# An encoder layer with product-key experts: both segments through one input stage, gathers behind it, half of the one-hot factors on ScalarE, a batched end

## The chip, the core and the metric

The kernel runs on one core of a Trainium2 chip. A core has five engines: PE (TensorE: matmuls; its weight loads are counted apart as PEld), DVE (VectorE), ACT (ScalarE), POOL (GpSimd) and SP (SyncE, which only issues DMAs here). Each engine takes its own instructions in order and waits for the others at semaphores; DMA engines move data beside them. The metric is device time of one execution in microseconds (us), as the median over runs.

## What is computed

One layer of an encoder over two groups of tokens with shared weights: a prompt of 512 tokens (four tiles of 128) and a sample of 256 (two tiles), D = 1024, all in float32.

```python
h = rmsnorm(x, norm1_g)
qa, ka, va, qg, kg, vg, rg, lr, gl = split_in_proj(einsum('bsd,de->bse', h, w_in))
ya = rmsnorm(diff_attention(qa, ka, va, lam, rel_bias)) @ w_up_a        # 4 heads
yb = (rmsnorm(gla forward + gla backward) * silu(rg)) @ w_up_b          # 4 heads, chunks of 64
gates = sigmoid(gl)                                                     # 2 branches
x = x + (gates[0] * ya + gates[1] * yb) @ w_out
x = x + peer_ffn(rmsnorm(x, norm2_g))
x = x + (p_i @ ple_w) * sigmoid(rmsnorm(x, norm3_g) @ ple_gate_w)
y = rmsnorm(x, final_norm_g)

def peer_ffn(h):                    # 8 heads; 128 x 128 = 16384 experts u, v of 1024
    s = (h @ w_q) . sub_keys        # 8 heads x 2 halves x 128 keys
    idx, top = the 16 best sums of the two halves, for each token and head
    act = gelu(u[idx] . h)
    return sum over the 8 x 16 choices of softmax(top) * act * v[idx]
```

## The kernel before

Float32 operands of the large products are split into a high and a low part (`split`: the high part is a copy on ACT, the low part a subtraction on DVE or POOL), and `mm3` (lines 176 to 178) makes each product of three matmuls: high by high, low by high, high by low. `wchunk` loads a weight chunk of 512 KB on SP's queue and splits it.

**Input stage, 0 to 944 us.** The sample goes first, alone: attention (`attention`, one head after the other), gated linear attention (`linear_attention`), `merge` (branch gates times the two branches), `out_proj`, `norm2`, `queries`. Then `choose` picks 128 experts for each of the sample's tokens (`select`, DVE almost alone), 352 to 398 us. Meanwhile PE makes 11 of the prompt's 16 branch gates (`branch_gate`, into tiles named fill), which go to DRAM and come back in `merge`. The prompt then takes the same way from 398 to 944: attention, linear attention, merge, out_proj, norm2 with the products of the per-layer inputs (`ple_products`), queries. So w_in (40 chunks) and w_up (8) are loaded and split twice. Splits of weights are shared between DVE and POOL.

**Sample experts: gathers.** For the sample's two tiles the chosen rows of u and v are fetched: 512 indirect DMAs of 128 rows each (`fetch`, line 703, issued by POOL, tile name row); DVE takes a dot product with each u row tile (line 725) and adds each v row tile (line 734). The generator `gg` yields after each fetch, and `pace(n)` takes it n steps on: calls of `pace` in other code set where the gathers stand. They begin under the prompt's attention.

**Prompt experts: two loops over all 16384 experts, dense.** First loop (64 chunks of 128 experts, 944 to 1480 us): `up` multiplies a chunk of u with the 512 tokens (24 matmuls into tile pa), `gelu` (line 996, ACT) makes act, which goes to DRAM (line 1010). Beside it `outer_products` builds a table of gates: for each token, L is the one-hot row of its 128 first indices and R the one-hot row of its second indices times the gate, both by comparison with iota on DVE (lines 949 and 954); L by R (line 957, tile po) gives 128 x 128 gates of one token, which ACT copies out (line 958). A step handles four tokens; an iteration takes two or three steps. Second loop (32 blocks of four chunks, 1480 to 2577 us): the other 64 chunks of u, and in eight groups a block the product of act times gates with v; each block's groups pace 11 gathers. Inside both loops the order on PE, DVE, ACT and POOL is the order in which the code is written (`manual_schedule`).

**End, 2577 to 2673 us.** `finish_all` multiplies by ple_gate_w, adds, normalizes (`rsqrt_mean`, a chain of small DVE instructions, once for each tile), scales (line 1102) and stores.

Of the kernel before, what the change touches and what calls it, by code (L numbers as in the profile page):

```python
# [16 lines left out]
P = 128  # L17
# [92 lines left out]
def build(tc, A, O):  # L110
# [8 lines left out]
    pss = tc.alloc_tile_pool(name="pss", bufs=2, space=PSUM, side="right")  # L119
# [4 lines left out]

    def side_tile():
        return ps2.tile([P, 2, 512], F32, name="side", bufs=1)

    def fill_tile():
        return pss.tile([P, 512], F32, name="fill", bufs=2)

    def pair_tile():
        return psb.tile([P, 2, 512], F32, name="pair", bufs=1)
# [21 lines left out]
    nw = [0]  # L154
    wf = None
    wx = tc.alloc_tile_pool(name="wx", bufs=1, side="right")

    def wchunk(src, eng=None, base=False, own=None):
        raw = (own or wp).tile([P, 8, P], F32, name="raw", bufs=2 if own else 3)
        nc.sync.dma_start(raw, src)  # L160
        nw[0] += base
        pool = own or (wx if base and nw[0] % 3 == 2 else wp)
        hi = pool.tile([P, 8, P], F32R, name="whi")
        lo = pool.tile([P, 8, P], F32R, name="wlo")
        split(hi, lo, raw, eng or G)
        return hi, lo

    def half_unit(src, k, base=False, dve=False):
        wh, wl = wchunk(src[:, 4 * k:4 * k + 4].rearrange("p a b -> p (a b)").rearrange("p (a b) -> p a b", b=P),
                        V if k or dve else G, base)  # L170
        return [a.rearrange("p a b -> p (a b)").rearrange("p (a b) -> p a b", b=256) for a in (wh, wl)]
# [27 lines left out]
    class Seg:  # L199
        def __init__(self, t0, nt, xT):  # L200
            self.t0, self.nt, self.n, self.xT = t0, nt, nt * P, xT
            self.tiles = list(range(t0, t0 + nt))

# [7 lines left out]
    def norm1(sg, pool):  # L211
        n = sg.n
        acc = pool.tile([P, n], F32, name="sqa", bufs=1)
        xc = pool.tile([P, 8, n], F32, name="xc", bufs=1)
        for c in range(0, 8, 2):
            nc.sync.dma_start(xc[:, c:c + 2], A[sg.xT][:, c:c + 2])
        for c in range(8):
            if c == 0:
                S.activation(acc, xc[:, c], AF.Square)
            else:  # L220
                sq = pool.tile([P, n], F32, name="sq", bufs=2 if n < 512 else 1)
                S.activation(sq, xc[:, c], AF.Square)
                V.tensor_add(acc, acc, sq)

        def finish():
            ps = mm_tile()[:, :n]
            if last_pe[0] is None:
                T.matmul(ps, ones, acc, start=True, stop=True)
            else:
                with tc.issue_after(last_pe[0].ins):  # L230
                    T.matmul(ps, ones, acc, start=True, stop=True)
            rs = rsqrt_mean(pool, ps, D, n, "n1", acc)
            for c in range(8):
                V.scalar_tensor_tensor(xc[:, c], xc[:, c], g1[:, c:c + 1], rs, op0=OP.mult, op1=OP.mult)
                split(sg.hT[0][:, c], sg.hT[1][:, c], xc[:, c], G if c % 3 == 2 else V)

        return finish
# [5 lines left out]
    hps = tc.alloc_tile_pool(name="hps", bufs=1)  # L243
    SS.hT = [hps.tile([P, 8, SS.n], F32R, name=n) for n in ("hsh", "hsl")]
    SP.hT = HP
    g1 = load("g1", [P, 8], A["g1"])
    lp = tc.alloc_tile_pool(name="ln", bufs=1)
    norm1(SS, lp)()
# [28 lines left out]
    wf = tc.alloc_tile_pool(name="wf", bufs=2, side="right")  # L277
    outer = tc.alloc_tile_pool(name="outer", bufs=1, side="right")
    SS.oa = [outer.tile([P, 4, SS.n], F32R, name="oa" + x) for x in "hl"]
    SS.ogl = outer.tile([P, 4, SS.n], F32R, name="ogl")  # L280
# [6 lines left out]
    nproj = [0]  # L287
# [15 lines left out]
    def attention(sg, mid=None):  # L303
        nt, n = sg.nt, sg.n
        op = tc.alloc_tile_pool(name="oat", bufs=1, reuse_waits="tile", side="right")
        onat = [op.tile([P, 4, P], F32, name=f"on{t}") for t in range(nt)]
        ssq = op.tile([P, nt, 4], F32, name="ssqa")
        with tc.tile_pool(name="at", bufs=2, reuse_waits="tile") as ap:
            for h in range(H):
                if h == MID and mid is not None:  # L310
                    mid()
                tb = ap.tile([P, W_TB], F32, name="tb")
                src = tbd[:, h]
                nc.sync.dma_start(tb, bass.AP(tensor=src.tensor, offset=src.offset + 127,
                                              ap=[[4 * 1024 - 1, P], [1, W_TB]]))

                o = proj(sg, 3 * h)
                qs = [ap.tile([P, n], F32R, name=f"qs{c}") for c in range(2)]
                for c in range(2):
                    hi, lo = HALF[c], HALF[1 - c]  # L320
                    S.activation(qs[c][hi], o[hi], AF.Copy, scale=0.125)
                    V.scalar_tensor_tensor(qs[c][lo], o[hi], 0.125, qs[c][hi].bitcast(F32),
                                           op0=OP.mult, op1=OP.subtract)
                o = proj(sg, 3 * h + 1)
# [59 lines left out]
    def linear_attention(sg, early, late):  # L384
        nt, n = sg.nt, sg.n
        nck = n // 64
        with tc.tile_pool(name="gl", bufs=2, reuse_waits="tile") as gp:
# [123 lines left out]
            for h in range(H):  # L511
                split(sg.og[0][:, h], sg.og[1][:, h], ogs[h])
# [690 lines left out]
```

## Time and profile before

| | |
|---|---|
| runs | 2674.69, 2660.84, 2669.11 us; median 2669.11 |
| profiled execution | 2674.42 us; its span 2672.7 us, mean granted clock 0.961 |
| PE busy | 2498.7 us (93%), 12640 records |
| DVE busy | 2106.7 us (79%) |
| ACT busy | 976.2 us (37%) |
| POOL busy | 832.0 us (31%) |
| moved by DMA | 622.57 MB, mean 233 GB/s |

The span is the time between the first and the last instruction of the profiled execution; about 2 us lie around it. Busy shares are means over stages that differ: what a stage is worth is read from that stage. The granted clock (PEclk) is the share of TensorE's full speed that the chip gave; 1.00 is 2.4 GHz, 0.50 is 1.2 GHz.

### The profile page before, as it was taken

The page shows a single profiled execution, that of the slowest core. Times are in us where ns is not written, and L with a number is a line of the kernel's source. Part 1 is how long each engine was busy: PE and PEld are TensorE (multiplying, and loading weights), DVE is VectorE, ACT ScalarE, POOL GpSimd, SP SyncE. Part 2 cuts the span into 40 slices and gives each one's busy share as a digit, 9 for nine tenths or more (in the row PEclk, how much of TensorE's full clock was granted, in tenths as well). Part 3 has the DMA queues.
Part 4 walks back from the last instruction along what each step waited for, and adds up shares of the span by engine and source line. Part 5 has one row for each costly group of instructions (what it writes and reads, how often), then busy time and mean ns, then how long its engine had stood idle before and what let it go on. Part 6 is the DMA issues. An engine that isn't in the chain of part 4 may idle for free.

```text
span 2672.7 us, 35759 instructions
## 1 busy us (share of the span) xinstructions
PE 2498.7 (93%) x12640; PEld 2064.1 (77%) x12640; DVE 2106.7 (79%) x4419; ACT 976.2 (37%) x1649; POOL 832.0 (31%) x682
## 2 busy tenths in 40 slices
PE   7899999999978969999999899999999999999995
PEld 5779987667775858778788688888888888887785
DVE  4755698896876799999877688888888888887365
ACT  6754425654233223333333322322222322223133
POOL 2224332341244301111111244444443544442100
PEclk9989999999987989999999899999999999999998
DMA  7325556673877237667677899999999999996231
GB/s 245 110 92 181 162 166 206 223 253 101 297 282 246 80 103 240 220 204 238 221 251 261 301 330 321 314 318 320 319 319 318 309 333 315 322 317 237 80 107 59
DMA packets 238340, 622.57 MB, mean 233 GB/s; under 512 B 20193, under 2 KB 90977, under 8 KB 235857
## 3 DMA queue, kind: packets, MB, share of 16 engines
q1 hardware_dynamic: 148304, 292.05, 34.4%
q0 software_dynamic: 73728, 268.47, 28.2%
q10 hardware_dynamic: 16128, 59.78, 5.8%
q8 instruction: 99, 1.62, 0.3%
q14 instruction: 81, 0.66, 0.1%
HBM read 557.30 MB, written 62.91 MB: 232 GB/s over the span
## 4 chain that ended last, share of the span: by engine, by line
PE 76%; DVE 16%; DMA 3%; issue 3%; ACT 2%; SPq 0%; POOL 0%; ACTq 0%; DVEq 0%; POOLq 0%
PE po L176 10%; PE po L178 10%; PE po L177 10%; PE pa L178 7%; PE pa L176 7%; PE pa L177 7%; PE mm L176 4%; PE mm L177 4%; PE mm L178 4%; PE po L957 3%; DVE R L954 1%; DVE side L734 1%; DVE wlo L985 1%; DVE eq L669 1%; DMA pr<-in_pT 1%
## 5 line engine op out<-in xcount | busy, mean ns | idle before, releaser
L703 POOL DMA_INDIRECT row<-in_v,idx x256 | 250.2, 977 | 744.6 <-DVE side L734 443.5
L178 PE MATMUL pa<-hh,wlo 128*128 128x512 f32 x1024 | 411.5, 402 | 18.2 <-DVE wlo L985 18.1
L176 PE MATMUL po<-vh,wth 128*128 128x512 f32 x1024 | 404.3, 395 | 13.5 <-ACT wth L150 12.8
L176 PE MATMUL pa<-hh,whi 128*128 128x512 f32 x1024 | 415.9, 406 | 0.0
L151 POOL TENSOR_TENSOR wlo<-raw,whi 128x1024 fp32r<-128x1024 f32 x125 | 303.1, 2427 | 348.5 <-ACT whi L150 264.3
L177 PE MATMUL pa<-hl,whi 128*128 128x512 f32 x1024 | 410.1, 401 | 0.0
L178 PE MATMUL po<-vh,wtl 128*128 128x512 f32 x1024 | 403.4, 394 | 0.0
L177 PE MATMUL po<-vl,wth 128*128 128x512 f32 x1024 | 402.8, 393 | 0.2 <-DVE vl L151 0.2
L703 POOL DMA_INDIRECT row<-in_u,idx x256 | 262.1, 1024 | 447.3 <-DVE gj L725 337.3
L734 DVE SCALAR_TENSOR_TENSOR side<-row,dots,side 128x1024 f32<-128x1024 f32 x256 | 328.5, 1283 | 11.9 <-DMA row<-in_v,idx 8.0
L150 ACT CAST whi<-raw 128x1024 fp32r<-128x1024 f32 x216 | 223.1, 1046 | 260.2 <-PE mm L177 99.7
L725 DVE SCALAR_TENSOR_TENSOR gj<-row,side 128x1024 bf16<-128x1024 f32 x256 | 310.9, 1214 | 3.5 <-DMA row<-in_u,idx 0.9
L150 ACT CAST vh<-raw 128x1024 fp32r<-128x1024 f32 x128 | 133.9, 1046 | 490.9 <-PE po L178 396.5
L178 PEld LDWEIGHTS pa<-hh,wlo 128*128 128x128 f32 x1024 | 195.7, 191 | 69.8 <-DVE wlo L985 22.4
L176 PEld LDWEIGHTS po<-vh,wth 128*128 128x128 f32 x1024 | 194.4, 190 | 57.8 <-ACT wth L150 16.7
L151 DVE TENSOR_TENSOR vl<-raw,vh 128x1024 fp32r<-128x1024 f32 x128 | 156.0, 1219 | 102.1 <-ACT vh L150 100.8
L177 PEld LDWEIGHTS pa<-hl,whi 128*128 128x128 f32 x1024 | 195.9, 191 | 44.9
L176 PEld LDWEIGHTS pa<-hh,whi 128*128 128x128 f32 x1024 | 196.3, 192 | 44.2
L178 PEld LDWEIGHTS po<-vh,wtl 128*128 128x128 f32 x1024 | 194.3, 190 | 42.9 <-DVE wtl L151 2.5
L177 PEld LDWEIGHTS po<-vl,wth 128*128 128x128 f32 x1024 | 194.5, 190 | 42.0 <-DVE vl L151 1.4
L1147 DVE TENSOR_TENSOR x<-x,po 128x512 f32<-128x512 f32 x256 | 173.7, 682 | 62.9 <-PE po L178 48.7
L996 ACT ACTIVATE act<-pa 128x512 f32<-128x512 f32 x128 | 76.0, 596 | 394.6 <-PE pa L178 394.6
(403 smaller groups left out, 4883.6 us busy)
## 6 DMA issues: line engine op xcount, KB each, us to landing
raw<-in_uT SPq DMA_DIRECT2D x128, 512.0 KB
raw<-in_v SPq DMA_DIRECT2D x128, 512.0 KB
raw<-in_w_in SPq DMA_DIRECT2D x80, 512.0 KB
gd<-blk ACTq DMA_DIRECT2D x16, 2048.0 KB
gr<-gd SPq DMA_DIRECT2D x32, 1024.0 KB
raw<-in_w_q SPq DMA_DIRECT2D x32, 512.0 KB
ad<-act ACTq DMA_DIRECT2D x64, 256.0 KB
ar<-ad SPq DMA_DIRECT2D x64, 256.0 KB
```

Of the source, the lines that this page charges most:

```text
L150: S.copy(hi, src)
L151: ins = (eng or V).tensor_sub(lo, src, hi.bitcast(F32))
L176: T.matmul(out, lh, rh, start=(i == 0), stop=False)
L177: T.matmul(out, lh, rl, start=False, stop=False)
L178: last_pe[0] = T.matmul(out, ll, rh, start=False, stop=(i == n - 1))
L669: V.tensor_tensor(eq, places[:, hf * Q:hf * Q + Q, None].to_broadcast([P, Q, 16]), marks[:, None, :].to_broadcast([P, Q, 16]), op=op)
L703: G.indirect_dma_start(out=r, out_offset=None, in_=A[table], in_offset=bass.IndirectOffsetOnAxis(ap=idx[:, k:k + 1], axis=0))
L725: V.scalar_tensor_tensor(jk, r, 1.0, hq, op0=OP.mult, op1=OP.mult, accum_out=dots[:, k:k + 1])
L734: V.scalar_tensor_tensor(acc, r, dots[:, k:k + 1], acc, op0=OP.mult, op1=OP.add)
L957: T.matmul(tp[:, k * P:(k + 1) * P], Rs[k], L[:, k], start=True, stop=True)
L996: S.activation(act, o, AF.Gelu_apprx_tanh)
L1147: V.tensor_add(x2[t][:, q], x2[t][:, q], o)
```

## The change

Sample and prompt share one input stage: `proj` takes the segments to which a chunk applies and yields one product for each, so each chunk of w_in and w_up is loaded and split once. Head 0 of attention runs for the sample alone while the prompt's first norm is made; heads 1 to 3, linear attention (two chains that alternate at `yield`) and merge take both. The branch gates are made inside `merge`, and the way through DRAM is gone. All weight splits ahead of the second loop are on DVE. The gathers begin behind `choose`, which now stands behind the sample's queries and the prompt's norm2: one step at each `ple_products` step (6) and each of the prompt's query chunks (16), one or two for each iteration of the first loop (96), 12 or 13 for each block of the second. In the first loop the R factors of every second token come from ACT, as Abs and then Relu, and a step handles eight tokens. At the end the square is taken one tile later, and the first five tiles share one reciprocal root and one round of stores.

The core of the diff (the segments' loops around it, and the same instructions written for either segment, are left out):

```diff
-    def wchunk(src, eng=None, base=False, own=None):
...
+    def wchunk(src, eng=None):
+        raw = wp.tile([P, 8, P], F32, name="raw", bufs=3)
         nc.sync.dma_start(raw, src)
...
-        split(hi, lo, raw, eng or G)
+        split(hi, lo, raw, eng or V)
...
-    def proj(sg, i):
-        nproj[0] += 1
-        wh, wl = wchunk(A["w_in"][i], V if sg is SP or nproj[0] % 2 else G, True)
-        o = projT(sg, wh, wl)
-        if sg is SP:
-            pace(PB)
-        return o
+    def proj(segs, i):
+        wh, wl = wchunk(A["w_in"][i])
+        for sg in segs:
+            yield sg, projT(sg, wh, wl)
...
+    def merge():
...
+                for b in range(2):
+                    for sg, o in proj(SEGS, 24 + 2 * j + b):
+                        th[sg, b] = mp.tile([P, sg.n], F32, name="gt", tag="gt" + sg.x, bufs=3)
+                        S.activation(th[sg, b], o, AF.Tanh, scale=0.5)
+                wh, wl = wchunk(A["w_up"][j])
...
     def queries(sg, hT, keys, tv, ti, qp, o_ps, s_ps):
...
-            wh, wl = wchunk(A["w_q"][j], V if sg is SS and j % 2 else G, True)
+            wh, wl = wchunk(A["w_q"][j])
...
+            if sg is SP:
+                pace(PQ)
...
-    for i in range(NF):
-        branch_gate(i, wf, fill_tile(), G, wf)
...
+    with tc.tile_pool(name="at0", bufs=2, reuse_waits="tile") as ap:
+        attn_head(0, (SS,), ap, 1)
+        with tc.tile_pool(name="lnp", bufs=1, reuse_waits="tile") as lp:
+            norm1(SP, lp)
+    with tc.tile_pool(name="at", bufs=2, reuse_waits="tile") as ap:
+        attn_head(0, (SP,), ap, 1)
+        for h in range(1, H):
+            attn_head(h, SEGS, ap, 1)
...
+    out_proj(SS, sqs, np_)
...
+    norm2(SS, sqs, np_, hg, tp_tile)
+    out_proj(SP, sqp, np_)
...
+        queries(SS, hg, keys, tvs, tis, qp, mm_tile, tp_tile)
...
+        norm2(SP, sqp, np_, HP, tp_tile)
...
+        for k, t in enumerate(SS.tiles):
+            choose(t, tvs, tis, k, qp)
...
+        for _ in ple_products(pp):
+            pace(1)
...
         queries(SP, HP, keys, tv, ti, qp, o_tile, o_tile)
...
         def outer_products(t):
...
-                for q in range(TB // 4):
...
+                for q2 in range(TB // 8):
+                    sets = []
+                    for q in (2 * q2, 2 * q2 + 1):
...
+                        for k in (1, 3):
+                            n = n0 + k
+                            Rs[k] = gb.tile([P, P], F32, name="R", bufs=RB)
+                            S.activation(Rs[k], iota, AF.Abs, bias=sT[:, 1, n:n + 1], scale=-1.0)
+                            S.activation(Rs[k], Rs[k], AF.Relu, bias=sT[:, 2, n:n + 1], scale=sT[:, 3, n:n + 1])
...
+                        for k in (0, 2):
...
+                            V.tensor_scalar(Rs[k], iota, sT[:, 1, n:n + 1], sT[:, 2, n:n + 1],
+                                            op0=OP.is_equal, op1=OP.mult)
...
-                advance(ga, 128 * (i - A0 + 1) // n - 128 * (i - A0) // n)
+                advance(ga, 64 * (i - A0 + 1) // n - 64 * (i - A0) // n)
...
-            pace(1)
+            pace(1 + i % 2)
...
-                if not pace(2 if g in (1, 4, 6) else 1):
+                if not pace(2 if g % 2 == 0 or g == 5 and b % 2 else 1):
...
                     if h:
                         if u == 3:
+                            store(0, NT - 1)
+                        square(NT - 1, u, cs)
+            store(NT - 1, 1)
```

How it moves instructions, first on ACT in the middle of the first loop. whi is the high part of the next chunk, pa the chunk's product, act its gelu, ad its place in DRAM, po the outer products, blk the table's block. Before:

```order
L996 ACTIVATE act<-pa 128x512
L1010 DMA ad_9295<-act 128x512
L958 COPY blk<-po 128x128x4 x2
L980 CAST whi<-raw 128x1024
L996 ACTIVATE act<-pa 128x512
```

and with the change (R: the factor, sT: the index, the gate and the negated gate of each token):

```order
L955 ACTIVATE act<-pa 128x512
L969 DMA ad_8422<-act 128x512
L900 ACTIVATE R<-iota,sT 128x128
L901 ACTIVATE R<-R,sT 128x128
L900 ACTIVATE R<-iota,sT 128x128
L901 ACTIVATE R<-R,sT 128x128
L900 ACTIVATE R<-iota,sT 128x128
L901 ACTIVATE R<-R,sT 128x128
L900 ACTIVATE R<-iota,sT 128x128
L901 ACTIVATE R<-R,sT 128x128
L917 COPY blk<-po 128x128x4 x2
L939 CAST whi<-raw 128x1024
```

Between the store of act and the copies there are now four pairs, each with its second instruction reading what the first one wrote.

Second, PE around the choices of the sample's experts. Before, behind the sample's queries (tp<-keys,pq are their last scores; fill is a prompt's branch gate):

```order
L176 MATMUL fill<-hh,whi 128x512
L177 MATMUL fill<-hl,whi 128x512
L178 MATMUL fill<-hh,wlo 128x512
L580 MATMUL tp<-keys,pq 128x128 x2
L176 MATMUL fill<-hh,whi 128x512
```

and with the change (mm<-hgh is the sample's last query chunk, tp<-ident,ht the transposes of the prompt's norm2, pwh, pwl and prh the parts of the per-layer input's product):

```order
L173 MATMUL mm<-hgh,wlo 128x256
L579 MATMUL tp<-keys,pq 128x128 x4
L569 MATMUL tp<-ident,ht 128x128 x32
L171 MATMUL mm<-pwh,prh 128x512
L172 MATMUL mm<-pwl,prh 128x512
```

Where the matmuls of the branch gates stood, there are now the transposes of norm2 and then at once the products of the per-layer inputs.

## Rows read from the trace of the kernel before

**Rows 1.** The page, part 4: the chain that ended last, by engine.

```profile
PE 76%; DVE 16%; DMA 3%; issue 3%; ACT 2%; SPq 0%; POOL 0%; ACTq 0%; DVEq 0%; POOLq 0%
```

**Rows 2.** Busy times by stretch (us, PE, PEld, DVE, ACT, POOL, PEclk, DMA share, GB/s).

```profile
0.00:944.00 944.00, 854.73 (x4824) 702.15 (x4825) 701.65 (x1903) 442.65 (x878) 313.32 (x234) 0.94 0.56 188
352.00:398.00 46.00, 42.28 (x174) 34.10 (x173) 46.00 (x219) 10.37 (x15) 23.52 (x13) 0.93 0.45 149
840.00:944.00 104.00, 103.71 (x500) 86.38 (x501) 74.81 (x456) 32.04 (x48) 32.38 (x15) 0.98 0.30 96
944.00:1480.00 536.00, 500.45 (x2605) 418.48 (x2604) 475.42 (x1230) 189.79 (x277) 71.35 (x71) 0.96 0.66 220
1000.00:1300.00 300.00, 284.85 (x1480) 237.42 (x1479) 287.44 (x736) 109.28 (x159) 37.47 (x39) 0.97 0.67 222
1300.00:1450.00 150.00, 150.00 (x818) 127.97 (x817) 116.62 (x251) 55.18 (x82) 22.45 (x21) 1.00 0.73 246
1530.00:2430.00 900.00, 899.25 (x3924) 736.78 (x3923) 764.81 (x979) 257.09 (x333) 413.55 (x354) 1.00 0.92 319
1700.00:1750.00 50.00, 50.00 (x221) 41.08 (x220) 43.96 (x70) 11.75 (x15) 28.70 (x25) 1.00 0.97 343
```

**Rows 3.** Time line of ACT, one iteration of the first loop (start, us, instruction, [idle]).

```profile
1103.25 0.60 ACT L996 ACTIVATE act<-pa 128x512 f32<-128x512 f32 x1 [5.38 <-PE pa L178]
1103.87 0.33 ACTq L1010 DMA_DIRECT2D ad<-act  x1
...
1110.65 0.60 ACT L996 ACTIVATE act<-pa 128x512 f32<-128x512 f32 x1 [4.09 <-PE pa L178]
```

**Rows 4.** Time line of PE in the same iteration.

```profile
1103.05 1.95 PE L957 MATMUL po<-L,R 128*128 128x128 f32 x16
1104.75 0.48 PE L176 MATMUL pa<-hh,whi 128*128 128x512 f32 x1
```

**Rows 5.** Groups of DVE by line, 944 to 1480 (busy us, mean ns | idle before).

```profile
L954 DVE TENSOR_SCALAR R<-iota,sT 128x128 f32<-128x128 f32 x512 | 142.0, 344 | 2.5 <-PE po L957 2.5
...
L734 DVE SCALAR_TENSOR_TENSOR side<-row,dots,side 128x1024 f32<-128x1024 f32 x63 | 80.7, 1281 | 0.0
L985 DVE TENSOR_TENSOR wlo<-raw,whi 128x1024 fp32r<-128x1024 f32 x63 | 76.9, 1221 | 41.4 <-ACT whi L980 41.3
```

**Rows 6.** Groups of ACT by line and shape, 0 to 944.

```profile
L495 ACT ACTIVATE jk<-tp 128x128 f32<-128x128 f32 x24 | 6.8, 283 | 0.0
...
L432 ACT ACTIVATE t<-mm,ab 128x512 f32<-128x512 f32 x4 | 2.7, 683 | 0.7 <-PE mm L429 0.5 <-DVE qe L451 0.2
...
L432 ACT ACTIVATE t<-mm,ab 128x256 f32<-128x256 f32 x4 | 1.9, 470 | 1.4 <-DVE qe L451 1.1 <-PE mm L429 0.3
```

**Rows 7.** Time line of ACT, two neighbours that do not depend on each other.

```profile
182.43 0.27 ACT L493 COPY gn<-tp 128x128 f32<-128x128 f32 x1
182.59 0.28 ACT L495 ACTIVATE jk<-tp 128x128 f32<-128x128 f32 x1
```

**Rows 8.** Instructions on gathered rows alone (us, DVE, POOL, PEclk, DMA share, GB/s).

```profile
0.00:944.00 944.00, 158.41 (x264) 144.24 (x131) 0.94 0.56 188
944.00:1480.00 536.00, 84.23 (x79) 70.58 (x66) 0.96 0.66 220
1480.00:2440.00 960.00, 398.83 (x445) 297.46 (x315) 0.99 0.92 319
```

**Rows 9.** Time line of PE after two waits, 533 and 614 to 619 us.

```profile
533.25 0.50 PE L176 MATMUL mm<-hh,whi 128*128 128x512 f32 x1 [1.27 <-ACT lrT L401]
...
614.60 0.50 PE L176 MATMUL mm<-hh,whi 128*128 128x512 f32 x1 [1.70 <-DVE silu L426]
614.93 0.40 PE L177 MATMUL mm<-hl,whi 128*128 128x512 f32 x1
...
619.28 0.39 PE L177 MATMUL mm<-hl,whi 128*128 128x512 f32 x1
```

**Rows 10.** Time line of ACT: scaling of the last tile of six, 5.41 us apart.

```profile
2667.80 0.72 ACT L1102 ACTIVATE x<-x,rs 128x512 f32<-128x512 f32 x1 [2.87 <-DVE rs L196]
```

More of the change, by code (lines that the diff above doesn't have):

```diff
@@ L276, in build @@
     lp.release()
[L277 to L280, printed above, removed]
     def projT(sg, wh, wl):
@@ new lines, in linear_attention @@
+                    vn = {}
+                    for sg, o in proj(SEGS, 16 + 2 * h):
+                        vT = gp.tile([P, sg.n], F32, name="vgT", bufs=1)
+                        S.copy(vT, o)
+                        vn[sg] = tile_(sg, "vgn", [P, sg.nt, P])
+                        to_natural(vn[sg], vT, sg.nt)
+                    for sg, ps in proj(SEGS, 17 + 2 * h):
+                        og = sg.silu[:, h]
+                        S.activation(og, ps, AF.Tanh, scale=0.5)
+                        V.scalar_tensor_tensor(og, og, 1.0, ps, op0=OP.add, op1=OP.mult)
@@ new lines, in linear_attention @@
+                    chains = [gla_head(sg, h, gp, tile_, lrT[sg], qd[sg, h], kd[sg, h], vn[sg], scm, ssq)
+                              for sg in SEGS]
+                    while chains:
+                        chains = [c for c in chains if next(c, True) is None]
+            rs = rsqrt_mean(gp, ssq.rearrange("p a b -> p (a b)"), P, NT * 4, "gl")
+            rs3 = rs.rearrange("p (a b) -> p a b", b=4)
+            ogs = {}
+            for sg in SEGS:
+                for t in range(sg.nt):
+                    V.tensor_mul(sg.gn[t], sg.gn[t], rs3[:, sg.r0 + t, :, None].to_broadcast([P, 4, P]))
+                for h in range(H):
+                    tp = tp_tile()
+                    for t in range(sg.nt):
+                        T.transpose(tp[:, t * P:(t + 1) * P], sg.gn[t][:, h], ident)
+                    ogs[sg, h] = tile_(sg, ("t0", "t1", "qe", "ke")[h], [P, sg.n])
+                    V.scalar_tensor_tensor(ogs[sg, h], tp[:, :sg.n], ggla, sg.silu[:, h], op0=OP.mult, op1=OP.mult)
@@ L777, in build @@
     LB = 4
[L778 to L802 removed]
+    RB = 10
+    PO = 1
+    PQ = 1
+    SEGS = (SS, SP)
+    oat = tc.alloc_tile_pool(name="oat", bufs=1, reuse_waits="tile", side="right")
+    ssqa = oat.tile([P, NT, 4], F32, name="ssqa")
+    for sg in SEGS:
+        sg.on = [oat.tile([P, 4, P], F32, name=f"on{sg.x}{t}") for t in range(sg.nt)]
     ggla = load("ggla", [P, 1], A["ggla"])
@@ L1132, in prepare, with four_groups @@
             return ws
+        def four_groups(ws):
+            os_ = [o_tile() for _ in range(4)]
+            for k, (th, tl, vh, vl) in enumerate(ws):
+                for g in range(4):
+                    r, q = slice(DEN[g // 2] * P, DEN[g // 2] * P + P), slice(g % 2 * 512, g % 2 * 512 + 512)
+                    T.matmul(os_[g], th[:, r], vh[:, q], start=(k == 0), stop=False)
+                    T.matmul(os_[g], tl[:, r], vh[:, q], start=False, stop=False)
+                    T.matmul(os_[g], th[:, r], vl[:, q], start=False, stop=(k == VB - 1))
+            return os_
         fresh = {}
```

665 lines of the change are left out of this document (297 added, 368 removed).

## The prediction

> **What bounds the kernel now.** I read the chain of waits first, then the busy times by stage, then time lines of single iterations. The chain is TensorE's (PE) for three quarters, VectorE (DVE) takes 16%, ScalarE (ACT) 2% [rows 1]: the question is where PE waits, and ACT has room on average. By stage [rows 2], the input stage (0 to 944 us) is busy for 854.7 us at a granted clock of 0.94; the first loop (944 to 1480) is nearly full, with DVE at 287.4 of 300 us in its middle; in the second loop PE is busy in 899.3 of 900 us, DVE in 764.8, with the DMA engines at 0.92. So a gain is possible only ahead of 1480 and in the last 100 us, and the second loop can only lose.
>
> In one iteration of the first loop [rows 3], 7.40 us lie from one gelu to the next. ACT needs 0.60 for the gelu and 0.33 to issue the store, then nothing that PE needs at once. PE has eight outer products ready when the chunk's matmuls end: they start at 1103.05, and the next chunk starts at 1104.75, 1.50 us after the gelu started [rows 3, 4]. PE does not stand still here, because the factors were made ahead on DVE. That is the place that the change touches most.
>
> **First loop.** It removes from DVE 256 of the 512 R factors (half of 142.0 us, 71 us) and puts 512 activations on ACT [rows 5]. The order of ACT settles what they cost: each step's eight activations stand behind the gelu, the gelu waits for the end of the chunk, and PE's outer products wait for the activations before the next chunk may start. So ACT's work moves from beside PE to the path. Half of the factors come from an engine that is idle on average, at the one moment when PE needs it.
>
> The pair: Abs with one pointer operand takes 470 ns on 256 columns and 683 on 512, so 0.83 ns a column and 364 ns on 128 [rows 6]. Relu here has two pointers; a 128-column activation without one takes 283 ns [rows 6], so a pointer is about 81 ns and the Relu 445. The Relu reads what its Abs wrote, so I let these two not overlap; neighbours that don't depend on each other start 0.16 us apart at 0.27 long, an overlap of 0.11 [rows 7]. A pair is 0.364 + 0.445 - 0.11 = 0.70 us. ACT is free 0.95 us after the gelu starts (1104.20); four pairs bring the last factor at 0.95 + 4 x 0.70 + 0.11 = 3.86, and one matmul (1.70 / 8 = 0.21) ends the step at 4.07 in place of 1.50: 2.57 us more in each of 64 steps, +165. The Trainium skill (ScalarE: Activation LUTs, What ACT_TABLE_LOAD costs) prices an activation at 186 ns and 0.833 ns a column, 93 ns for each pointer, 93 ns of overlap; by it the pair is 0.77 us, and the sum would be 18 us more than by the rows. No table load is added: Abs and Relu follow a Tanh without one before, and both orders hold 30 loads.
>
> Given back is what DVE costs PE now: at the pace of 1300 to 1450 (818 matmuls in 150.0 us) the 1480 of 1000 to 1300 would take 271 us, so 29 go. DVE keeps 71 us less of factors and gets 30 more gathers (96 against 66) of some 1.28 us [rows 5, 8], 38 us, so it stays clear. Together +136. Bounds: if all eight activations stream 0.16 apart the last is there at 0.95 + 7 x 0.16 + 0.28 = 2.35, which makes +1.06 a step, +68 - 29 = +39; without overlap, and 0.1 us for each hand-over, the pair is 0.91 and the step +3.30, +211 with nothing given back. I take +136, since the first row of the pair is the same function with the same kind of operand.
>
> **Clock.** PE's first new wait in a step ends with the first pair, 0.95 + 0.81 = 1.76 us after the gelu starts, less one DVE-made product: about 1.6 us of idling in each iteration. A gap of 1.27 us was followed by matmuls at full clock, one of 1.70 by 12 steps in 4.35 us (614.93 to 619.28) [rows 9], where (7.40 - 1.70) / 24 = 0.237 us each gives 2.84: 1.5 us lost at the lower level of 1.2 GHz. 1.6 lies between the two gaps, so I charge half of the 61 iterations: +45, between 0 and +92.
>
> **Input stage.** Each w_in and w_up chunk is loaded and split once for both segments (48 loads of 512 KB fewer; also the 16 gates' way through DRAM and back), and 109 of 131 gathers leave 0 to 944 (131 there now [rows 8], 22 in the new order). They took 158.4 us of DVE and 144.2 of POOL; the splits that POOL did come to DVE, 1.22 us each [rows 5]. PE's own matmuls stay, so what can come back is its idle time, 944 - 855 = 89 us, and the clock's, 0.06 x 944 = 57 us, some 50 of it in matmuls: 140 at most. Most waits in the heads are chains through ACT and DVE that two interleaved segments cover only in part; I take half, -70. Against it stand three new waits. In 352 to 398 DVE works on the two choices for 46.00 us while PE fills 42.28 us of it with prompt gates [rows 2]; now nothing of PE's stands there but products that need a split queued behind the choices on DVE: +42, bare. In the prompt's queries DVE has 74.8 of 104 us; 16 splits (1.22) and 16 gathers (1.28) make it 115: +12. The sample's queries get 8 splits: +2. Sum -14, from -84 (all back) to +56 (nothing).
>
> **Second loop.** Gathers rise from 315 to 394, over 1097 us rather than 960: 9% more a microsecond. DMA share 0.92 becomes about 0.97, DVE's 0.85 about 0.89. At 0.97 (1700 to 1750) PE was busy in 50.00 of 50 us [rows 2], so this is nearly hidden: 0 at best; at worst one gather step of 1.28 us late in each of 32 blocks, +41, since the POOL split of the next chunk stands behind one gather more. I take +10, a quarter of that.
>
> **End.** The last tiles each wait 2.87 us for a reciprocal root [rows 10]; six become two: -12 (-8 to -15).
>
> **Sum:** 136 + 45 - 14 + 10 - 12 = +165 on the profiled 2674.4, so 2839. That execution lies 5 us above the median of 2669.1, so **2834 us** against the median, 6% slower.
>
> **Rivals.**
> *The input stage pays (faster).* PE becomes the bound from 0 to 944 and gives back all of it: -84. For: DVE loses 158 us of gathers there, PE's idle time is scattered through it, and the interleaving is aimed at the same waits. Against: the bare choices. It decides if the activations are cheap: 64 x (4 x pair - 0.23) - 29 - 84 - 2 is zero at a pair of 0.51 us, between my 0.70 and the 0.32 of neighbours. At 0.40 it is -27: 2642 us. Chance 0.12.
>
> *The clock falls in every iteration (slower still).* For: the gap of 1.70 that is followed by a fall. If the fall is as short as there, 61 x 1.5 = +92 in place of 45; if a whole chunk runs at the lower level, its 24 matmuls cost 5.7 us more, 61 x 5.7 = +348. Against: gaps up to 1.27 pass without one. Between these ends about 2950 us. Chance 0.16. The Trainium skill (TensorE: Matmul & The Clock Gate, A second HAM failure mode: psum-queue depth-cycling) describes a kernel whose short idling between groups of matmuls made the clock swing between its two levels; the trace shows falls behind single gaps, but no loop that repeats one, and by that page this rival would be the likelier one.
>
> *The second loop is bound by gathers.* DVE or DMA at their limit for part of the time: +41 in place of 10, with the rest as forecast: 2865. For: 0.92 is close. Against: 0.97 passed. Chance 0.06.
>
> *The factors' wait is hidden.* PE would need other work between a chunk and its products; the order shows none. With input as forecast the total would be -29 - 14 + 10 - 12, about 2624. Chance 0.01. Between the cases, an input gain that just pays for cheap activations, within 0.5% (some 13 us, about what this measurement can tell from no change): 0.05.
>
> **How the numbers follow.** The forecast keeps 0.60. Slower is forecast, clock and gathers, 0.82; same 0.05; faster 0.12 + 0.01. The forecast's own bounds: a cheap pair (-97) with half of the input's remaining gain (-35) is 132 below it, a dear pair (+75) with every clock fall (+47) 122 above, 2702 to 2956; the top goes on to where the second rival's middle lies. So the range is **2700 to 2980**, which leaves out most of the first rival and the upper end of the second.
>
> **What would show it.** Right: in the first loop a step of about 10 us from gelu to gelu, with PE waiting some 2 us for ACT's R in each; pairs of 0.7 us; PE nearly still for 40 us at the choices; the input stage ending close to 944; the second loop as long as before, at a DMA share near 0.97; two waits for a root at the end. Wrong: a first loop under 560 us (activations cheap or covered), an input stage under 880, PE gaps in the second loop, or a granted clock under 0.8 in the first loop, which would be the second rival.

## The result and the profile after

The changed kernel takes 2983.39 us (2982.25 to 2983.52, 4 runs) against 2666.16 of the kernel before (2660.84 to 2674.69): ratio 1.1186, 95% interval 1.1153 to 1.1218, 317 us slower. The direction was forecast; the size, 165 us, was half of it, and 2983 lies 3 us above the range. The profiled execution of the changed kernel has a span of 2980.5 us, 308 more than the 2672.7 of the kernel before; the profiles divide these 308 us.

The chain that ended last (page, part 4) now has 12% of "issue" and 8% of ACT; in [rows 1] these were 3% and 2%:

```profile
PE 61%; DVE 14%; issue 12%; ACT 8%; DMA 3%; POOL 2%; ACTq 1%; SPq 0%; POOLq 0%; DVEq 0%
```

Busy times by stretch of the changed kernel (us, PE, PEld, DVE, ACT, POOL, PEclk, DMA share, GB/s), which answer to [rows 2]: the input stage, in it linear attention, the choices, the products of the per-layer inputs and the prompt's queries, then the first and the second loop:

```profile
0.00:1000.00 1000.00, 864.62 (x4828) 708.66 (x4829) 556.88 (x1651) 395.88 (x829) 30.93 (x58) 0.91 0.27 86
233.20:469.80 236.60, 202.22 (x1084) 155.03 (x1082) 114.64 (x240) 111.16 (x246) 5.38 (x19) 0.84 0.10 30
802.00:850.00 48.00, 7.20 (x29) 5.05 (x28) 47.27 (x229) 6.57 (x12) 6.85 (x7) 0.55 0.24 80
850.00:895.00 45.00, 22.79 (x71) 14.95 (x71) 23.97 (x33) 10.36 (x18) 2.39 (x3) 0.76 0.40 133
895.00:1000.00 105.00, 104.11 (x504) 85.50 (x505) 94.75 (x461) 30.84 (x46) 14.34 (x18) 1.00 0.48 165
1000.00:1769.00 769.00, 600.13 (x2631) 475.58 (x2629) 471.23 (x1138) 390.74 (x789) 100.43 (x100) 0.91 0.53 176
1769.00:2892.00 1123.00, 1070.63 (x4596) 870.23 (x4596) 961.98 (x1195) 312.90 (x406) 528.96 (x454) 0.97 0.91 320
```

Here the first loop ends with its last chunk matmul and the second with its last product with v. By the same marks the loops of the kernel before end at 1487 and 2570 (not 1480 and 2577, as above):

```profile
944.00:1487.00 543.00, 507.45 (x2634) 424.13 (x2633) 475.42 (x1230) 189.79 (x277) 71.35 (x71) 0.96 0.66 220
1487.00:2570.00 1083.00, 1065.21 (x4598) 867.47 (x4597) 869.27 (x1103) 307.81 (x403) 447.29 (x377) 0.98 0.85 293
```

So the 308 us lie in four places. The input stage ends at 1000 instead of 944 (+56). The first loop takes 769 instead of 543 (+226). The second loop lasts 1123 where it was 1083 (+40). From there to the end it is 89 against 103 (-14). The number of PE's records is the same (12640 in both); its waits and its clock changed.

An iteration of the first loop, ACT's time line of the changed kernel (start, us, instruction, [idle before]), against [rows 3]:

```profile
1303.55 0.60 ACT L955 ACTIVATE act<-pa 128x512 f32<-128x512 f32 x1 [4.26 <-PE pa L173]
1304.18 0.33 ACTq L969 DMA_DIRECT2D ad<-act  x1
1304.55 0.40 ACT L900 ACTIVATE R<-iota,sT 128x128 f32<-128x128 f32 x1 [0.40 <-DVE wlo L944]
1304.99 0.49 ACT L901 ACTIVATE R<-R,sT 128x128 f32<-128x128 f32 x1
1305.39 0.39 ACT L900 ACTIVATE R<-iota,sT 128x128 f32<-128x128 f32 x1
...
1307.44 0.49 ACT L901 ACTIVATE R<-R,sT 128x128 f32<-128x128 f32 x1
1307.85 1.26 ACT L917 COPY blk<-po 128x512 f32<-128x512 f32 x2
...
1314.13 0.60 ACT L955 ACTIVATE act<-pa 128x512 f32<-128x512 f32 x1 [4.08 <-PE pa L173]
```

and PE in the same iteration, against [rows 4]:

```profile
1303.35 0.38 PE L914 MATMUL po<-L,R 128*128 128x128 f32 x2
1305.53 2.95 PE L914 MATMUL po<-L,R 128*128 128x128 f32 x14 [1.80 <-ACT R L901]
1308.23 0.48 PE L171 MATMUL pa<-hh,whi 128*128 128x512 f32 x1
```

From gelu to gelu it is 10.58 us, 7.40 before. ACT stands idle for 4.1 to 4.3 us while PE works on the chunk, then does 3.4 us of factors while PE waits: after one product PE idles 1.80 us for the first pair, and the next chunk starts 4.68 us after the gelu instead of 1.50. PE's waits by cause, 984 to 1782 us (total, times, longest), have one leader:

```profile
PE po L914 <- ACT R L901: 118.4, 62, 2.6
```

### The profile page after: what moved, and what is told of

It is laid out like the page before. It is cut to its first block, busy times and chain, and to the rows that moved or that the text cites. A ratio compares the mean times of both kernels' runs of the same rounds, so it can differ in the third digit from the quotient of the medians.

```text
span 2980.5 us, 35546 instructions
## 1 busy us (share of the span) xinstructions
PE 2606.8 (87%) x12640; PEld 2124.9 (71%) x12640; DVE 2041.7 (69%) x4112; ACT 1133.9 (38%) x2112; POOL 660.3 (22%) x611
## 4 chain that ended last, share of the span: by engine, by line
PE 61%; DVE 14%; issue 12%; ACT 8%; DMA 3%; POOL 2%; ACTq 1%; SPq 0%; POOLq 0%; DVEq 0%
PE po L171 7%; PE po L173 7%; PE po L172 7%; PE pa L171 6%; PE pa L172 6%; PE pa L173 6%; PE mm L171 3%; PE mm L172 3%; PE mm L173 3%; ACT R L901 2%; POOL row L704 2%; PE po L914 2%; DVE wlo L153 1%; ACT R L900 1%; DVE gj L726 1%
## 5 line engine op out<-in xcount | busy, mean ns | idle before, releaser
L704 POOL DMA_INDIRECT row<-in_u,idx x256 | 251.9, 984 | 1004.1 <-DVE gj L726 724.6
L171 PE MATMUL pa<-hh,whi 128*128 128x512 f32 x1024 | 428.4, 418 | 0.0
L171 PE MATMUL po<-vh,wth 128*128 128x512 f32 x1008 | 397.7, 395 | 24.5 <-ACT wth L152 18.0
L172 PE MATMUL pa<-hl,whi 128*128 128x512 f32 x1024 | 418.2, 408 | 0.0
L173 PE MATMUL po<-vh,wtl 128*128 128x512 f32 x1008 | 396.3, 393 | 0.1
L153 DVE TENSOR_TENSOR wlo<-raw,whi 128x1024 fp32r<-128x1024 f32 x109 | 132.8, 1220 | 279.4 <-ACT whi L152 276.0
L914 PE MATMUL po<-L,R 128*128 128x128 f32 x1024 | 205.2, 328 | 133.4 <-ACT R L901 118.4
L152 ACT CAST whi<-raw 128x1024 fp32r<-128x1024 f32 x171 | 176.5, 1047 | 304.5 <-PE mm L172 160.7
L914 PEld LDWEIGHTS po<-L,R 128*128 128x128 f32 x1024 | 160.3, 215 | 180.7 <-ACT R L901 174.1
L171 PEld LDWEIGHTS pa<-hh,whi 128*128 128x128 f32 x1024 | 203.7, 199 | 45.6
```

What stands on the lines that cost most here:

```text
L152: S.copy(hi, src)
L153: ins = (eng or V).tensor_sub(lo, src, hi.bitcast(F32))
L171: T.matmul(out, lh, rh, start=(i == 0), stop=False)
L172: T.matmul(out, lh, rl, start=False, stop=False)
L173: last_pe[0] = T.matmul(out, ll, rh, start=False, stop=(i == n - 1))
L704: G.indirect_dma_start(out=r, out_offset=None, in_=A[table], in_offset=bass.IndirectOffsetOnAxis(ap=idx[:, k:k + 1], axis=0))
```

## The experiments

**One: the factors back on DVE.** Nothing else is undone; steps of eight tokens and the ring of ten tiles stay.

```diff
-                        for k in (1, 3):
...
-                            S.activation(Rs[k], iota, AF.Abs, bias=sT[:, 1, n:n + 1], scale=-1.0)
-                            S.activation(Rs[k], Rs[k], AF.Relu, bias=sT[:, 2, n:n + 1], scale=sT[:, 3, n:n + 1])
...
-                        for k in (0, 2):
+                        for k in range(4):
```

> The changed kernel with all four R factors of a group made on VectorE again; the step of eight tokens, the ring of ten R tiles and everything else stay. Theory W (ScalarE's eight activations stand between the gelu and PE's products, so their 3.3 us are on the path in every step): an iteration goes from 10.58 back to some 7.4 us, the first loop from 768 to 545 to 580 us (VectorE then has about 542 us of work in it), total 2983 down to 2770 to 2810 us. Rival (the step of eight tokens and the smaller ring hold PE up, whoever makes the factors): iteration stays above 9.5 us, total above 2930 us.

Measured: 2776.35 us, 207 less than the changed kernel. The first loop is down to 568 us although DVE is busy in 518 of them (e1_dve by stretch):

```profile
999.00:1567.00 568.00, 513.96 (x2628) 427.52 (x2626) 517.90 (x1394) 189.49 (x277) 101.68 (x100) 0.95 0.70 240
```

So the step of eight, the ring and the 30 gathers more account for at most the 25 us that are left to the 543 before; no run separates them.

**Two: the same activations, ahead of the gelu.** The generator yields between factors and products, and the factors of a step are asked for before the gelu is written.

```diff
                         sets.append((q, L, Rs))
+                    yield
                     tps = []
...
+            if m:
+                advance(ga, 1)
             act = gelu(o)
             nc.scalar.dma_start(ad[i // VB][:, i % VB], act)
...
+                advance(ga, 2 * m - 1)
```

> The changed kernel with the same 512 activations, but each step's factors are written ahead of the gelu, into the 4 us in which ScalarE waits for the chunk; the products stay behind the gelu. Theory W (the place of the activations, not their number): iteration 7.4 to 7.6 us, no wait of PE for R, granted clock of the first loop back from 0.91 to 0.96 or more, total 2745 to 2790 us. Rival (ScalarE's throughput or VectorE's operand sharing: the activations are too much work wherever they stand): iteration above 9 us, total above 2880 us.

Measured: 2765.98 us, 217 less than the changed kernel with the same 512 activations. ACT's time line (e2_ahead) shows the first and the last of the eight in the hole that was idle, and the gelu 7.41 us after the one before:

```profile
1065.53 0.60 ACT L956 ACTIVATE act<-pa 128x512 f32<-128x512 f32 x1 [0.80 <-PE pa L173]
...
1068.75 0.40 ACT L900 ACTIVATE R<-iota,sT 128x128 f32<-128x128 f32 x1
...
1071.64 0.49 ACT L901 ACTIVATE R<-R,sT 128x128 f32<-128x128 f32 x1
1072.94 0.60 ACT L956 ACTIVATE act<-pa 128x512 f32<-128x512 f32 x1 [0.80 <-PE pa L173]
```

So it was where the work stood, not how much. The loop takes 557 us, though, not less than the 543 before. Against experiment one, which has the same steps and gathers, what DVE gave up bought 11 us.

**Three: half of ACT's work left out.** Without the Relu the factors are not the one-hot rows.

```diff
-                            S.activation(Rs[k], Rs[k], AF.Relu, bias=sT[:, 2, n:n + 1], scale=sT[:, 3, n:n + 1])
```

> The changed kernel without the second activation (the Relu that turns the distance into the gate) of each ScalarE factor: this part of the one-hot factors is left out. Theory W: 4 x 0.41 = 1.64 us less in each of 64 steps, -105 us, and up to 45 more where PE's first wait of 1.80 us falls to 1.39 and the granted clock no longer falls: 2830 to 2880 us. Rival (PE pays for the handovers from ScalarE, not for its work): less than 30 us, above 2950 us.

Measured: 2856.32 us, 127 less. The usual iteration falls from 10.58 to 8.94 us: 105 us in 64 steps. That this is the 4 x 0.41 of my expectation is luck: the four Abs alone take 1.28 us where the eight activations took 3.38, so ACT became 2.10 us shorter, and 1.64 of it reached PE (e3_norelu, ACT):

```profile
1105.48 1.28 ACT L900 ACTIVATE R<-iota,sT 128x128 f32<-128x128 f32 x4 [0.40 <-ACT act L954]
```

The other 22 are mostly clock. PE's waits in the two kinds of iteration (e3_norelu; in every fourth, ACT also issues a store of the table between gelu and factors):

```profile
1105.93 1.83 PE L913 MATMUL po<-L,R 128*128 128x128 f32 x14 [1.27 <-ACT R L900]
...
1133.22 1.83 PE L913 MATMUL po<-L,R 128*128 128x128 f32 x14 [1.76 <-ACT R L900]
```

In none of the 51 iterations that have one of these waits and no other does the clock fall. In the changed kernel the two waits are 1.80 and 2.28 us. Behind 1.80, in the iteration shown above, the chunk's matmuls start 0.23 to 0.24 us apart; behind this 2.28 they do not (PE, changed kernel):

```profile
1104.85 3.25 PE L914 MATMUL po<-L,R 128*128 128x128 f32 x14 [2.28 <-ACT R L901]
...
1108.33 0.63 PE L172 MATMUL pa<-hl,whi 128*128 128x512 f32 x1
1108.76 0.63 PE L173 MATMUL pa<-hh,wlo 128*128 128x512 f32 x1
...
1110.38 0.40 PE L171 MATMUL pa<-hh,whi 128*128 128x512 f32 x1
```

They stand 0.43 us apart, the level of 1.2 GHz, until 1110.38. The longer wait comes with the 0.46 us that ACT's queue needs for the store at 1103.37. But its length alone does not decide: elsewhere in the same loop the clock falls behind 1.80 (matmuls 0.43 us apart) and stays up behind 2.28 (0.23):

```profile
1388.18 3.25 PE L914 MATMUL po<-L,R 128*128 128x128 f32 x14 [1.80 <-ACT R L901]
...
1391.66 0.63 PE L172 MATMUL pa<-hl,whi 128*128 128x512 f32 x1
...
1554.92 2.95 PE L914 MATMUL po<-L,R 128*128 128x128 f32 x14 [2.28 <-ACT R L901]
...
1557.94 0.40 PE L172 MATMUL pa<-hl,whi 128*128 128x512 f32 x1
```

Of the changed kernel's 55 iterations with no other wait, 24 contain a stretch at the lower level: 10 of the 14 with the longer wait (2.28 to 2.57) and 14 of the 41 with 1.80. Such an iteration is 0.6 to 1.4 us longer than one with the same wait and no fall, some 26 us together.

**Four: 32 gathers more in the first loop.**

```diff
-            pace(1 + i % 2)
+            pace(2)
```

> The changed kernel with two gathers in every iteration of the first loop instead of one and two in turn: 32 gathers come out of the second loop. Theory D (the 15.4 and 3.1 us that PE waits at 2820 us for the last tile's transposes are gathers that were not done when the loop ended): these waits go, the second loop ends 15 to 20 us earlier, total 2963 to 2970 us. Rival (that wait is the normal finishing of the last tile, as the 4 us in the kernel before, or the gathers cost the first loop as much): total within 5 us of 2983.

Measured: 2958.69 us, 25 less, a little more than the 13 to 20 expected. In the changed kernel PE waited at the end of the second loop for the last gathered rows, twice, before it could turn the sample's tiles (PE):

```profile
2834.99 1.94 PE L569 MATMUL pt<-ident,h 128*128 128x128 f32 x8 [15.43 <-DVE h L996]
2840.01 1.94 PE L569 MATMUL pt<-ident,h 128*128 128x128 f32 x8 [3.07 <-DVE h L996]
```

With 32 fewer gathers in the second loop (e4_pace2) the first of these is 4.97 us and the second is gone, as in the kernel before, where PE waited 4.1 us there:

```profile
2764.11 1.94 PE L569 MATMUL pt<-ident,h 128*128 128x128 f32 x8 [4.97 <-DVE h L996]
```

and the first loop is about as long as it was, 772 us.

**Five: the kernel before without fill work.** One number: none of the prompt's gates is made early.

```diff
-    NF = 11
+    NF = 0
```

> The kernel before, with none of the prompt's 16 branch gates as fill work (11 of them were): all are made at the end of the prompt's linear attention. Theory C (the input stage of the change is slower because gates that filled PE's waits have gone, not because the segments are merged): the choices stand bare, 38 to 42 us, and the fills that lay in other waits come back on the path, together 40 to 65 us more before the first loop, total 2708 to 2735 us. Rival (the merging itself, or the splits that left POOL, makes the input stage slower): less than 15 us, total below 2685 us.

Measured: 2719.12 us, 52 more than the kernel before (ratio 1.0193, 1.0159 to 1.0228), without any merging. PE now waits through the choices as in the changed kernel (e5_nofill, PE):

```profile
402.10 0.77 PE L340 MATMUL pair<-kd,qs 128*128 128x512 f32 x1 [45.39 <-DVE qs L322]
```

The changed kernel has the same hole, in two pieces (PE):

```profile
849.03 0.79 PE L171 MATMUL mm<-pwh,prh 128*128 128x512 f32 x1 [33.22 <-ACT prh L152]
863.81 0.80 PE L172 MATMUL mm<-pwl,prh 128*128 128x512 f32 x1 [13.98 <-DVE pwl L153]
```

The first names ACT, whose casts (pwh, prh) are short; in its queue they stood behind the second choice's exponential, which had waited for DVE (ACT):

```profile
847.22 0.31 ACT L693 ACTIVATE g<-g 128x128 f32<-128x128 f32 x1 [22.10 <-DVE g L692]
...
848.37 0.61 ACT L152 CAST prh<-pr 128x512 fp32r<-128x512 f32 x1
```

**Six: the end alone,** `finish_all` of the changed kernel in the kernel before.

```diff
+                        if k:
+                            square(k - 1, u, cs)
...
+                            store(0, NT - 1)
+                        square(NT - 1, u, cs)
+            store(NT - 1, 1)
```

> The kernel before with the changed end alone (square one tile later, first five tiles share one root and one round of stores). Forecast of the sum: four waits of 2.87 us for a root go, -12 us (-8 to -15), total 2652 to 2660 us against some 2668. Rival (the stores at once cost as much as the roots did): within 3 us of the kernel before.

Measured: 2653.97 us, ratio 0.9953 (0.9931 to 0.9976), 13 us less. Six waits of 2.87 us for a root [rows 10] are two; ACT's time line of the changed kernel shows the same pair:

```profile
2969.43 2.19 ACT L1041 ACTIVATE x<-x,rs 128x1024 f32<-128x1024 f32 x2 [3.40 <-DVE rs L191]
2974.89 0.72 ACT L1038 ACTIVATE x<-x,rs 128x512 f32<-128x512 f32 x1 [2.87 <-DVE rs L191]
```

**Seven: gates inside linear attention.** Eight of the 16 gates of both segments are made between the steps of the chains and kept in DRAM until merge.

```diff
                     while chains:
                         chains = [c for c in chains if next(c, True) is None]
+                        step += 1
+                        if step in (2, 4):
+                            early_gate()
```

> The changed kernel with 8 of the 16 branch gates of both segments made between the steps of the linear attention's chains, and kept in DRAM until merge. Theory C (PE idles 31.6 us and runs at a granted clock of 0.85 in the 227 us of linear attention because nothing of its own fills the chains): that stretch grows by less than the gates' 8 x 24 x (0.236 + 0.125) = 69 us which leave merge, total 2983 down to 2938 to 2960 us. Rival (the chains are bound by VectorE and ScalarE, which the gates also need): less than 10 us.

Measured: 2952.68 us, 31 less (two runs, 12.6 us apart); in the trace the input stage ends at 970 instead of 1000. Linear attention (e7_gates) takes 268 us instead of 237. One gate of each segment already stood there in the changed kernel, so seven more, 7 x 24 x 0.361 = 61 us of matmuls, went in for 31, and the clock there is 0.94 instead of 0.84:

```profile
231.00:499.00 268.00, 243.45 (x1418) 193.48 (x1416) 124.26 (x247) 124.73 (x268) 5.26 (x19) 0.94 0.17 54
```

**Eight: the choices between the query chunks.**

```diff
             if sg is SP:
-                pace(PQ)
+                advance(picks, 2)
...
-            pace(1 + i % 2)
+            pace(2)
```

> The changed kernel with the choices of the sample's experts taken in steps between the prompt's query chunks, the products of the per-layer inputs ahead of them, no gather before the first loop and two in each of its iterations. To be held against e4_pace2 (2958.7 us), which also has two. Theory C (the 47 us in which PE waits behind the choices are a matter of order): PE's wait goes, VectorE in the prompt's queries gets 47 us of choices for 20 us of gathers and becomes the bound there by some 15 us, total 2915 to 2940 us. Rival (VectorE's work only moves the wait into the queries): total above 2950 us.

Measured: 2947.09 us, 12 less than e4_pace2, short of what I expected and between the two ranges. The hole of 47 us is gone, but the first loop starts at 996 us, 2 earlier than in e4_pace2. The rival was the right one for this stage: the queries take 145 us instead of 105, and PE waits in them for splits that queue behind choices (e8_cover, PE's waits from 800 to 1000, and the stretch):

```profile
PE po L173 <- DVE wlo L153: 31.6, 3, 17.2
```

```profile
851.00:996.00 145.00, 110.41 (x502) 89.06 (x503) 122.96 (x615) 31.38 (x47) 0.14 (x1) 0.89 0.18 58
```

The choices are DVE's work: beside queries whose splits are DVE's too they did not hide, beside gates with their splits on POOL, in the kernel before, they did. Of the 12 us some 5 lie in the first loop; the rest I did not follow up.

**Nine: the kernel before with the changed outer products alone** (the diff of `outer_products` and its calls, and RB).

> The kernel before with the changed outer products alone (half of the R factors on ScalarE behind the gelu, steps of eight tokens, ring of ten); input stage, gathers and end as before. Theory W: an iteration goes from 7.41 to 10.6 us, the first loop from 536 to 755 to 775 us, total 2880 to 2910 us: this part alone is some 230 of the change's 317 us. Rival (the first loop's loss needs the change's other parts, its two gathers an iteration or the splits on VectorE): total below 2840 us.

Measured: 2891.43 us, ratio 1.0843 (1.0807 to 1.0879), 224 more. The wait is the same without the rest of the change (e9_factors, PE, 944 to 1710):

```profile
PE po L968 <- ACT R L955: 118.0, 62, 2.5
```

**Ten: three edits together** in the changed kernel: two, four and seven.

> The changed kernel with three edits together: factors ahead of the gelu (e2_ahead, -217), two gathers in every iteration of the first loop (e4_pace2, -25), eight gates inside linear attention (e7_gates, -31). If these are separate places on the path they add: 2710 us (2700 to 2730), still above the kernel before, by the bare choices (47 us). Rival (they share a cause, so part is counted twice): above 2740 us. Other rival (one chunk load for both segments pays once the covers are back): below 2670 us.

Measured: 2716.78 us, ratio 1.0188 (1.0158 to 1.0218). The single edits add to 273 us, together they gave 267: three separate places on the path. What is left to the kernel before is not the bare choices alone, though the 49 us are near their 47: between the profiled executions, 43 us apart, the input stage is 26 us longer (it ends at 970), the first loop 20 (563 against 543), the second 11, and the end is 14 shorter.

**Eleven: gathers off one short stretch of the kernel before.** On top of six, the gathers between the prompt's norm2 and its queries go (27 by the calls of `pace`, not the 30 of my expectation), 16 of them into the queries.

```diff
-    norm2(SP, sq, np_, HP, tp_tile, lambda: pace(PB))
+    norm2(SP, sq, np_, HP, tp_tile)
     for _ in ple:
-        pace(PB)
+        pass
...
+            if sg is SP:
+                pace(1)
```

> The kernel before with the batched end (e6_end, 2654 us) and one more piece of the change's idea in small: no gather between the prompt's norm2 and its queries (30 were, in 60 us in which PE idles 24.7 us and VectorE is busy 47.3), one behind each of the 16 query chunks, where VectorE has 29 us to spare; the other 14 run on at the end of the second loop, where gathers were done 130 us before the end. Theory G (those gathers delay the chain of norm2 and the per-layer products on VectorE): that stretch gets 10 to 20 us shorter and the queries no longer, total 2634 to 2646 us. Rival (the stretch waits for its own chain of transposes, splits and loads, not for the gathers): within 4 us of 2654.

Measured: 2628.29 us, ratio 0.9849 (0.9833 to 0.9866) to the kernel before, faster than both kernels. The stretch from 780 to 840 became 38 us and the queries 102, fully busy (e11_later, against the kernel before):

```profile
775.00:813.00 38.00, 25.93 (x103) 18.44 (x102) 21.95 (x36) 15.61 (x29) 3.33 (x2) 0.87 0.47 154
813.00:915.00 102.00, 102.00 (x502) 85.11 (x501) 84.71 (x477) 29.49 (x44) 43.59 (x26) 1.00 0.43 149
```

```profile
780.00:840.00 60.00, 35.34 (x102) 23.68 (x101) 47.34 (x80) 16.06 (x29) 25.88 (x25) 0.66 0.81 274
```

So moving gathers behind a stage paid where that stage waited for DVE. The gain, 26 us on top of six, is above the expectation (10 to 20 from this stretch, which gave 22).

## Why the prediction was wrong, step by step

On the profiled executions the forecast was +165 and the measurement +308. The 143 us between them are 70 of the input stage, 45 of the first loop, 30 of the second and -2 of the end.

**First loop: mechanism right, sum too small (+181 forecast with the clock, +226 measured).** Experiments one, two, three and nine show the mechanism: ACT's factors behind the gelu, on PE's path. The term that was mis-sized is the pair. I took 0.70 us, with an overlap at one of its two joints. It measures 0.82 to 0.84: the Relu starts 0.42 to 0.44 after its Abs, which is 0.39 to 0.40 long, and the next Abs 0.40 after a Relu of 0.49. Each step grew by 3.18 us, not 2.57: 203 against 165 in 64 steps. The Trainium skill (ScalarE: Activation LUTs, What ACT_TABLE_LOAD costs) would have given 0.77 and 18 us more than my rows. The trace lies above it: the lengths agree (0.39 and 0.49 us, where an estimate from that section's figures gives 386 and 479 ns), and its overlap of 93 ns is seen behind the Relu and not behind the Abs, whose result the Relu reads.

The 29 us "given back" were not. Experiment two makes the same iteration of 7.41 us as before and leaves DVE its relief, and the loop still takes 557. The slow iterations of the kernel before were those of the prompt's choices; they wait for a chain of DVE instructions, and that chain is not shorter when DVE has less beside it: PE's longest wait in them, for the index i1f, is 2.1 us in the kernel before and up to 2.9 in e2_ahead. I had read a full DVE (287.4 of 300 us, [rows 2]) as a bound.

The clock cost less than the +45 charged. The count was near my half of the iterations (24 of the 55 plain ones), but a fall cost 0.6 to 1.4 us and not 1.5: some 26 us, and the 22 of experiment three fit that. Steps and clock make 203 + 26 = 229 of the measured 226.

**Input stage: the step that failed (-14 forecast, +56 measured).** The step is the -70, half of PE's idle time and of the clock's, that was to come back. Little of it came back. PE's idle time in the stage rose from 89 us (944 - 855) to 135 (1000 - 865), and for as many matmuls it was busy 10 us longer, at a granted clock of 0.91 instead of 0.94: together the 56. Of the 46 us of idle time, 35 lie at the choices, norm2 and the products of the per-layer inputs (63.0 us idle from 802 to 895, 28.4 before in 352 to 398 and 780 to 840) and 10 in linear attention. In all the rest PE idled for 38 us where it had idled for 37: there, two segments in one stage covered no more than one after the other. Why they did not, no run shows. (The same input stage ended at 938 and 935 in the traces of e6_end and e9_factors, so the +56 may be some us too small.)

Of the three waits set against the -70, the bare choices (+42) came as priced, 33.2 and 14.0 us, and the queries came cheaper (105 against 104 us, not +12). What I missed is a second cover. I looked for the gates only in 352 to 398, where they show as fill; they lay elsewhere too. This is the tile fill alone in the kernel before (us, PE, PEld, ACT, PEclk, DMA share, GB/s):

```profile
116.00:232.00 116.00, 18.30 (x45) 10.84 (x45) 0.60 (x1) 0.91 0.35 112
232.00:352.00 120.00, 12.91 (x45) 8.71 (x46) 1.19 (x2) 0.99 0.55 171
```

and these are its two stretches of linear attention, with all that PE did there:

```profile
97.00:232.00 135.00, 122.35 (x863) 107.90 (x862) 79.27 (x143) 81.96 (x164) 41.05 (x26) 0.91 0.34 106
532.00:677.20 145.20, 133.55 (x680) 100.97 (x681) 118.86 (x223) 74.42 (x147) 39.46 (x46) 0.95 0.54 183
```

These 280 us also held the sample's 16 gates (16 x 24 x 0.125 = 48), 45 fill matmuls (11) and five of the prompt's gates (5 x 24 x 0.237 = 28), and 36 matmuls of linear attention ran ahead of them (7): 200 us without gates, by this estimate. The changed kernel's linear attention takes 237 us, one gate of each segment in it (9), so 228 without, with PE idle for 34.4 of the 237 at a clock of 0.84. That is some 28 us, and experiment seven took 31 back by putting half of the gates there again. With the 47 for the choices the new waits were about 75 us instead of the 56 in my sum; less the 56 measured, that leaves some 19 given back, where I had counted on 70. About 12 of the 19 are idle time at norm2 and the per-layer products, which the gathers left, as they do in experiment eleven (47 us of new waits there, but only 35 of new idle time). Experiment five shows the bare choices on the kernel before, without merging.

**Second loop (+10 forecast, +40 measured).** That more gathers are hidden in its middle was right: e4_pace2 kept a DMA share of 0.96 over its second loop up to 2770, and that loop is 23 us shorter than the changed kernel's. But I priced only delays inside blocks. The loop before ended its gathers some 125 us before its own end; 392 instead of 315 (instructions on gathered rows alone, changed kernel, against [rows 8]) used that margin up, and 18.5 us of drain stood bare, where it had been 4.1:

```profile
1769.00:2892.00 1123.00, 503.04 (x540) 379.31 (x392) 0.97 0.91 320
```

Experiment four took this back and left 17 of the 40 us, among them a longer wait for wth behind the first loop (13.2 us, 6.8 before). What causes these I did not follow up.

**End (-12 forecast, -14 measured):** -13 by experiment six.

**The rivals.** "The input stage pays" was refuted where it was to show: PE was not the bound there. "The clock falls in every iteration" gave a time near the measured one by the wrong way: the first loop's clock is 0.91, it falls in 24 of 55 plain iterations, and the falls are about a tenth of the loop's loss. The Trainium skill (TensorE: Matmul & The Clock Gate, A second HAM failure mode: psum-queue depth-cycling), by which I had called that rival the likelier one, is borne out in kind, since the clock does swing in this loop, but not in size: some 26 us, not 92 or more.

**The range** failed by 3 us because its upper end summed a dear pair and clock falls, and left the input stage and the second loop at their middle. Those sums give 2956, and the second rival's middle was given as about 2950; the 2980 follows from neither, and that the time came within 3 us of it is chance. The first loop, the input stage and the second loop were all off to the same side.

## What to carry to other kernels

An engine that is idle 60% of the time can still be the path: before work is moved to it, look in its time line at the moment at which the waiting engine needs the result, and write the work into the hole ahead of that moment (217 us here, for a change of order). When a stage is rebuilt, list every place where its independent work used to fill another engine's wait, by tile and over the whole span; where that work goes, those waits come bare. Work that is paced through a loop needs the margin at the loop's end checked as well as the room in its middle.

## What was not expected of the hardware

The length of PE's wait did not by itself tell whether TensorE's clock falls. With a wait of 1.80 us in an iteration of 10.58 us it fell in 14 of 41 iterations, with 2.28 to 2.57 in 10 of 14; with 1.27 or 1.75, in e3_norelu, in none of 51; in the kernel before it fell behind a single 1.70 [rows 9]. What else decides, no run here shows. And two neighbouring activations of 128 columns, the second reading the first's result on the same engine, start 0.44 us apart at a length of 0.40, whereas the next, which reads nothing of theirs, starts 0.09 us before the end of its forerunner; in e3_norelu, where each of the four reads nothing of the others', all four take 1.28 us.
